# Strassen weight sums on VectorE one at a time, two products accumulated in PSUM, norm weights spread by TensorE: one step of a hybrid encoder on one core

## The chip, the cores and the metric

The kernel runs on one core of a Trainium2 chip. The metric is the device time of one execution in microseconds (us), as a median over runs. A core has engines with instruction queues of their own, which work in order and wait for each other by semaphores: TensorE (PE, matrix products into PSUM), VectorE (DVE), ScalarE (ACT), GpSimd (POOL), and SyncE (SP), which here only issues DMAs from the chip's memory (HBM) to the on-chip memory (SBUF).

## The reference

One inference step of two layers for 512 prompt tokens and 8 x 16 sample tokens, 640 in all, each of 1024 features. Per layer, cut to what matters here:

```python
h = rmsnorm(x) * g_norm[l, 0]
a_x, ..., pu = split(h @ w_in[l])            # four mixers: conv, two attentions, pooling -> o_a .. o_d
for i, o_i in enumerate((o_a, o_b, o_c, o_d)):
    merged += sigmoid(h @ w_gate[l, i] + b_gate[l, i]) * (o_i @ w_branch[l, i])
x = x + rmsnorm(merged @ w_out[l]) * g_norm[l, 1]
gu = (rmsnorm(x) * g_norm[l, 2]) @ w_ffn_in[l]               # 1024 x 5632
x = x + rmsnorm((silu(gu[:, :2816]) * gu[:, 2816:]) @ w_ffn_out[l]) * g_norm[l, 3]
```

All data are fp32.

## The kernel before

**Products in parts.** Every matrix is split in a high and a low part (`split`, `copy` and `sub`), and a product is three matmuls: high x high, high x low, low x high (`dense_k`). A weight chunk arrives by a DMA that SP issues (`w_dma`, two raw tiles of 128x1032 in turn); `w_split` has ScalarE copy the high part (`whi`, L117), and puts the subtraction that gives the low part (`wlo`) in a list, which `flush` gives to VectorE (L274). `whi` and `wlo` have four buffers each, and `w_sub` runs two pieces ahead of the piece that TensorE takes.

**Strassen.** Two stages multiply 2x2 blocks with seven products in place of eight: one of the four gates (`strassen_gates`, four steps n a layer) and the FFN's first matrix (`strassen`, steps j = 3 to 21, 19 a layer; j = 0 to 2 run as plain dense products). A step's blocks are 512 weights x 320 tokens; `product` is 12 matmuls of 320 columns. The weight side needs four sums of blocks for a step: `weight_sums` (L446) forms them on GpSimd, 46 times four in all, one step ahead. The token side needs sums of quadrants, formed once per stage by `token_sums` on VectorE, in ten forms per half; these are put off by `after(delay, ...)` and come out one by one as `tick` counts the matmuls' progress. For the gates they are begun in `prepare_gates` at `f == GATE_F` with the step `GATE_STEP`. The results of a step's products are put together by VectorE's `add`s (L1844 in the FFN, L1538 in the gates), which read one product in PSUM each; ScalarE then applies tanh or Silu.

**Order.** The program's order per engine is the order in which the Python code issues it (`manual_schedule`), so every engine's queue is written out by hand through generators and the hooks named above. Temporary tiles `s` come from 33 slots (`NSLOT`, `alloc`, `free`). PSUM has pools `psD` (two tiles of two banks), `psS` (two), `psT` and `psO` (one each).

**Starts.** `ab_start` begins a dense stage with two chunks whose tokens are not all ready: first the tokens up to `CUT` for both chunks, then those from `CUT`; `hooks` call at a given k of the first halves. It runs four times (input projection and FFN-in of both layers). The very first (`first`) normalises tile by tile of 128 tokens: `norm1` (ScalarE's squares, L344; GpSimd's root, L338; VectorE's scaling by the root and the norm weights g, L353) and `norm2` (TensorE's transposes, L361; ScalarE's high part `Ph`; VectorE's low part `Pl`, L120). The norm weights are brought to all 128 partitions by two DMAs (`load_g`).

Of the kernel before, what the change touches and what calls it, by code (L numbers as in the profile page):

```python
# [25 lines left out]
HT = T // 2  # L26
CUT = 384
NEG = -1e30
BIG = 3.0e38
NSLOT = 33  # L30
ORDER = [0, 1, 2, 3, "v", 4, 5, 6, 7, 12, 13, 9, 10, 14, 11, 15, 8]
# [6 lines left out]
J0 = 3  # L38
GATE_F = 3
GATE_STEP = 0.8  # L40
FO_ORDER = (4, 0, 1, 2, 3, 5, 6, 7, 8, 9, 10)
# [19 lines left out]
def encoder_step(ctx: ExitStack, tc: tile.TileContext, I, O):  # L61
    nc = tc.nc
# [293 lines left out]

    def norm2(xn, hi, lo, t):
        for h in range(2):
            ps = psS()
            for c in range(4):  # L360
                PE.transpose(ps[:, c * 128:(c + 1) * 128], xn[h][:, c * 128:(c + 1) * 128], ident)  # L361
            pv = ps.rearrange("p (c n) -> p c n", c=4)
            split(hi[:, 4 * h:4 * h + 4, t * 128:(t + 1) * 128], lo[:, 4 * h:4 * h + 4, t * 128:(t + 1) * 128], pv)
            free(xn[h])
# [26 lines left out]

    def ab_start(keys, x, hooks, evac_fn):
        w = []
        Ds = [psD(), psD()]
        for i in range(2):
            w.append([w_sub(keys[i], p, 0) for p in range(2)])
            if i == 0:
                w_split(sidx[keys[1], 1])
                flush()
            dense(Ds[i], w[i], x, (0,), hooks[i])  # L400
        for i in range(2):
            dense(Ds[i], w[i], x, (1,))
            evac_fn(i, Ds[i])
            if i == 0:
                w_ahead(keys[1], 1)
                flush()
# [8 lines left out]

    x_first = [load_x(I["x"], t) for t in range(2)]
    g_first = load_g(0, 0)
    ident = const("ident", C_ID, 128)
    mhalf = cpool.tile([128, 8], F32, tag="mhalf", name="mhalf")
    G.memset(mhalf, -0.5)  # L420
# [23 lines left out]
    wsum = {}  # L444

    def weight_sums(key, blocks):  # L446
        a11, a12, a21, a22 = blocks
        s1, s2, s3, s4 = (alloc() for _ in range(4))
        for o, x, y, op in ((s1, a21, a22, ALU.add), (s2, s1[:, :512], a11, ALU.subtract), (s3, a11, a21, ALU.subtract),
                            (s4, a12, s2[:, :512], ALU.subtract)):  # L450
            G.tensor_tensor(out=o[:, :512], in0=x, in1=y, op=op)  # L451
        wsum[key] = (s1, s2, s3, s4)

# [9 lines left out]
    def token_sums(h, dst, at, step=0.6):  # L463
# [12 lines left out]
        def form(n, q):  # L476
            if n == 0:
                t[q] = [alloc() for _ in range(4)]
            i, a, b, op = steps[n]
            o = v2(t[q][i])  # L480
            a = o if a is None else v2(t[q][a]) if isinstance(a, int) else quad(0, *a, q)
            b = v2(t[q][b]) if isinstance(b, int) else quad(*b, q)
            V.tensor_tensor(out=o, in0=a, in1=b, op=op)
            if n == len(steps) - 1:
                t["formed"] = q
# [510 lines left out]
    def layer(l, Htag, Otag, hT, first_units):  # L996
# [471 lines left out]

        def gate_sums(p):
            if p < 4:  # L1470
                weight_sums(("gs", l, p), [t[:, :512] for t in gq["blk", p]])

# [13 lines left out]
        def prepare_gates(f):  # L1486
            if f == 2:
                load_gates(0)
            elif f == GATE_F:
                gq["t2"] = {}  # L1490
# [12 lines left out]
            elif f == 7:  # L1503
                gate_sums(0)
                need(lambda: gq["t"].get("formed") == 1)
# [5 lines left out]
        def strassen_gates(br, branch):  # L1511
# [11 lines left out]

            def product(ps, n, p):
                wh, wl = w_sub(("gs", l, n), p)
# [3 lines left out]
                for k in range(4):  # L1529
                    a, b = wh[:, k * 128:(k + 1) * 128], wl[:, k * 128:(k + 1) * 128]  # L1530
                    for pi, (w, x) in enumerate(((a, xh), (a, xl), (b, xh))):
                        PE.matmul(ps[:, :HT], w, x[k], start=(k == 0 and pi == 0), stop=(k == 3 and pi == 2))  # L1532
                    if k == 1:
                        yield
# [13 lines left out]
            for n in range(4):  # L1548
                f = 2 * n
                ta, tb, X, Y = alloc(), alloc(), alloc(), alloc()  # L1550
                s1, u2, u3, c22 = X[:, :HT], X[:, HT:], Y[:, :HT], Y[:, HT:]
                yield from product(psO(), n, 0)
                copy(s1, out["p"])
# [10 lines left out]
                if pend:  # L1564
                    branch(f - 1, [pend[1]])
                    yield
                yield from product(psT(), n, 3)
                add(c22, out["p"], u3)
                add(u2, out["p"], u2)
                tanh(tb, 1, c22, f + 1)  # L1570
                gate_sums(n + 1)
                yield
                yield from product(psD()[:, 0, :], n, 4)
                add(s1, out["p"], s1)
                tanh(ta, 0, s1, f)
                yield
                yield from product(psD()[:, 0, :], n, 5)
                add(u3, u3, out["p"], ALU.subtract)
                tanh(tb, 0, u3, f + 1)
                yield  # L1580
                yield from product(psS(), n, 6)
                add(u2, out["p"], u2)
                tanh(ta, 1, u2, f)
                post.append(lambda X=X, Y=Y: free(X, Y))
                pend = [ta, tb]
                yield
            for fn in post:
# [197 lines left out]

        def sums(j):
            if j < NJ:
                weight_sums(("fs", l, j), blocks_of(j))

# [18 lines left out]
        for j in range(1, J0):  # L1808
            for g in range(2):
# [4 lines left out]
                if j == J0 - 1 and g == 0:  # L1814
                    sums(J0)
                ev_fi(j, g, Dt)
# [8 lines left out]

        def product(ps, j, p):
            wh, wl = w_sub(("fs", l, j), p)
            xh, xl = moving[p]
            for k in range(4):
                a, b = wh[:, k * 128:(k + 1) * 128], wl[:, k * 128:(k + 1) * 128]  # L1830
                for pi, (w, x) in enumerate(((a, xh), (a, xl), (b, xh))):
                    PE.matmul(ps[:, :HT], w, x[k], start=(k == 0 and pi == 0), stop=(k == 3 and pi == 2))  # L1832
                if k == 1:
# [4 lines left out]
        def strassen(j):  # L1838
# [6 lines left out]

            p1 = product(psO(), j, 0)
            for fn in tail[:1]:
# [8 lines left out]
            add(u3, p7, u2)  # L1856
            sums(j + 1)
            p5 = product(psT(), j, 3)
            add(c22, p5, u3)
            add(u2, p5, u2)  # L1860
            p2 = product(psD()[:, 0, :], j, 4)
            add(s1, p2, s1)
            A.activation(out=act[:, :HT], in_=s1, func=AF.Silu)  # L1863
            p4 = product(psD()[:, 0, :], j, 5)
# [3 lines left out]
            add(act[:, :HT], act[:, :HT], s1, ALU.mult)  # L1868
            p3 = product(psS(), j, 6)
            add(u2, p3, u2)  # L1870
# [59 lines left out]
    with tc.manual_schedule():  # L1930
        h0 = (big("Ph"), big("Pl"))

        def first(evac_fn):
            xn = {}
            turned = lambda t: norm2(xn.pop(t), h0[0], h0[1], t)
            def normed(t):
                xn[t] = norm1(x_first[t], g_first)
                free(*x_first[t])

            normed(0)  # L1940
            normed(1)
            turned(0)
            normed(2)
            turned(1)
            w_split(1)
            flush(G)
            turned(2)
            normed(3)

            def mid():  # L1950
                normed(4)
                turned(3)

            ab_start([("in", 0, c) for c in ORDER[:2]], h0, ({4: mid}, {6: lambda: turned(4)}), evac_fn)
            free(*g_first)
# [154 lines left out]
```

## Time and profile before

| | |
|---|---|
| median of 3 runs | 2091.82 us (2089.9 to 2094.06) |
| the profiled execution's own time | 2095.22 us |
| its span, first to last instruction | 2093.4 us |
| mean granted TensorE clock | 0.993 of full |
| TensorE busy | 2038.4 us (97%) |
| VectorE busy | 1491.2 us (71%) |
| ScalarE busy | 981.7 us (47%) |
| GpSimd busy | 429.6 us (21%) |
| HBM traffic | 101 GB/s over the span |

The busy shares say how much of the span an engine worked; a view of waits says for which instruction of which engine it stood idle. In a row, `wlo<-raw,whi` reads: tile `wlo` is written from `raw` and `whi`; buffer numbers are left out. The gates' Strassen stages lie near 476 to 560 us (layer 0) and 1511 to 1590 (layer 1), the FFN's of layer 1 from 1694 to 1934.

### The profile page before, as it was taken

What the parts mean: (1) busy time and instruction counts of PE and PEld (TensorE: products, weight loads), DVE (VectorE), ACT (ScalarE), POOL (GpSimd) and SP (SyncE); (2) the same over time, 40 slices, a digit from 0 to 9 for tenths busy, and PEclk for the clock granted to TensorE, in tenths of its full rate; (3) what the DMA queues carried; (4) which work ended last, traced back from release to release, by engine and by line L of the source; (5) the groups of instructions that cost most, each with busy time, mean ns of one, the idle gap of its engine ahead of it and who ended that gap; (6) DMA issues with size and microseconds to landing.
All of it is one profiled execution on the core that took longest, in us unless ns stands there. A gap on an engine that the chain in (4) does not pass through costs nothing. (4 is left out here: it accounts for less than half of the span.)

```text
span 2093.4 us, 34625 instructions
## 1 busy us (share of the span) xinstructions
PE 2038.4 (97%) x13050; PEld 1928.6 (92%) x13050; DVE 1491.2 (71%) x2914; ACT 981.7 (47%) x2100; POOL 429.6 (21%) x450
## 2 busy tenths in 40 slices
PE   7999999998999999999999999999999999999998
PEld 7999999998989999988889999999988899999887
DVE  5687478698769889853375774876986698888432
ACT  5656355554444344343256553555544443444431
POOL 3211000113013444400040100001130234443000
PEclk9999999999999999999999999999999999999999
DMA  4312244342341222222523122444313422221223
GB/s 148 109 62 79 81 146 140 119 134 73 102 168 62 91 88 84 81 81 71 171 82 110 68 77 82 151 151 141 111 46 130 153 71 90 88 82 61 101 91 121
DMA packets 100743, 214.35 MB, mean 102 GB/s; under 512 B 10896, under 2 KB 35056, under 8 KB 100576
## 3 DMA queue, kind: packets, MB, share of 16 engines
q1 hardware_dynamic: 99552, 209.16, 29.9%
q0 software_dynamic: 1024, 2.98, 0.4%
q8 instruction: 102, 1.67, 0.3%
q14 instruction: 65, 0.53, 0.1%
HBM read 196.02 MB, written 16.08 MB: 101 GB/s over the span
## 5 line engine op out<-in xcount | busy, mean ns | idle before, releaser
L274 DVE TENSOR_TENSOR wlo<-raw,whi 128x512 fp32r<-128x512 f32 (+2 forms) x388 | 267.5, 694 | 160.0 <-ACT whi L117 155.5
L117 ACT ACTIVATE whi<-raw 128x512 fp32r<-128x512 f32 (+2 forms) x390 | 230.5, 606 | 168.6 <-issue 70.6
L274 DVE TENSOR_TENSOR wlo<-s,whi 128x512 fp32r<-128x512 f32 x196 | 205.3, 1048 | 17.5 <-ACT whi L117 16.1
L117 ACT ACTIVATE s<-s 128x512 fp32r<-128x512 f32 (+7 forms) x294 | 175.0, 619 | 77.6 <-DVE s L1420 45.6
L376 PE MATMUL D<-Ph,whi 128*128 128x320 f32 (+2 forms) x736 | 176.9, 315 | 0.9 <-DVE s L1412 0.9
L376 PE MATMUL D<-Qh,whi 128*128 128x320 f32 (+2 forms) x736 | 176.0, 313 | 0.9 <-DVE s L1412 0.9
L376 PE MATMUL D<-Pl,whi 128*128 128x320 f32 (+2 forms) x736 | 173.6, 310 | 0.0
L376 PE MATMUL D<-Ph,wlo 128*128 128x320 f32 (+2 forms) x736 | 173.6, 310 | 0.0
L376 PE MATMUL D<-Qh,wlo 128*128 128x320 f32 (+2 forms) x736 | 172.8, 309 | 0.0
L376 PE MATMUL D<-Ql,whi 128*128 128x320 f32 (+2 forms) x736 | 172.8, 309 | 0.0
L117 ACT ACTIVATE whi<-s 128x512 fp32r<-128x512 f32 x196 | 117.2, 621 | 42.2 <-PE S L1832 18.9
L338 POOL TENSOR_TENSOR r<-ms,mhalf 128x1 f32<-128x1 f32 x40 | 22.0, 551 | 542.1 <-DVE ms L1672 470.4
L376 PEld LDWEIGHTS D<-Ph,whi 128*128 128x128 f32 x736 | 123.0, 189 | 3.6 <-DVE s L1412 1.4
L376 PEld LDWEIGHTS D<-Pl,whi 128*128 128x128 f32 x736 | 125.2, 189 | 0.6 <-DVE Pl L120 0.4
L376 PEld LDWEIGHTS D<-Qh,whi 128*128 128x128 f32 x736 | 122.5, 188 | 3.4 <-DVE s L1412 1.5
L376 PEld LDWEIGHTS D<-Ql,whi 128*128 128x128 f32 x736 | 124.7, 188 | 0.2
L376 PEld LDWEIGHTS D<-Ph,wlo 128*128 128x128 f32 x736 | 124.8, 189 | 0.0
L376 PEld LDWEIGHTS D<-Qh,wlo 128*128 128x128 f32 x736 | 124.3, 188 | 0.0
L744 POOL CAST s<-s 128x16 fp32r<-128x16 f32 x128 | 30.8, 264 | 407.5 <-DVE s L1420 98.2
L451 POOL TENSOR_TENSOR s<-V,V 128x512 f32<-128x512 f32 x48 | 76.1, 1584 | 172.5 <-DMA V<-in_w_fi 85.3
L117 ACT ACTIVATE s<-T 128x320 fp32r<-128x320 f32 (+6 forms) x132 | 50.9, 386 | 106.5 <-PE T L515 62.5
L1863 ACT ACTIVATE s<-s 128x320 f32<-128x320 f32 x38 | 17.9, 472 | 148.4 <-DVE s L1844 148.4
(480 smaller groups left out, 5890.5 us busy)
## 6 DMA issues: line engine op xcount, KB each, us to landing
raw<-in_w_gate SPq DMA_DIRECT2D x48, 512.0 KB, 3.6
raw<-in_w_fi SPq DMA_DIRECT2D x48, 512.0 KB, 3.5
raw<-in_w_fo SPq DMA_DIRECT2D x44, 512.0 KB, 3.5
V<-in_w_fi SPq DMA_DIRECT2D x80, 256.0 KB, 3.0
raw<-in_w_in SPq DMA_DIRECT2D x32, 512.0 KB, 3.3
s<-in_ck_d SPq DMA_DIRECT2D x32, 256.0 KB, 4.1
s<-in_cv_d SPq DMA_DIRECT2D x32, 256.0 KB, 4.1
s<-in_ck_f SPq DMA_DIRECT2D x32, 256.0 KB, 4.1
```

The source lines that it names most:

```text
L117: A.activation(out=out, in_=in_, func=AF.Copy, scale=scale)
L274: E.tensor_tensor(out=lo, in0=raw, in1=hi, op=ALU.subtract)
L338: G.tensor_tensor(out=out, in0=ssum, in1=mhalf[:, :n], op=ALU.pow)
L376: PE.matmul(Dt[:, h, :c1 - c0], a, b[:, k, c0:c1], start=(start and pi == 0), stop=(stop and pi == 2))
L451: G.tensor_tensor(out=o[:, :512], in0=x, in1=y, op=op)
L744: G.tensor_copy(out=dst[:, 512:KEYS], in_=f32(src[:, 16 * b:16 * b + 16]))
L1863: A.activation(out=act[:, :HT], in_=s1, func=AF.Silu)
```

## The change

1. `weight_sums` becomes `weight_sum(key, blocks, i)`: one sum at a time, on VectorE. In the FFN they are issued behind the adds of products p7 and p5, behind the product p2 and the adds of p4; those of the first step j = 3 are put off by `after(1.0 + i)` within the last dense chunk before. In the gates they come behind products 3 to 6, and the first step's four at `f == 7`.
2. Product 4 is accumulated onto product 0 in the `psO` tile, and product 6 onto product 3 in the `psT` tile. In each step two adds go, and ScalarE reads PSUM for one half.
3. In `first` the norm weights of layer 0 come as two rows of 2 KB, issued by ScalarE's queue; a memset of `ones` and two matmuls spread them into a `psD` tile `gp`. Tiles 0 and 1 are scaled from `gp`; ScalarE copies it to SBUF for the rest. The order of tiles, transposes and weight splits changes.
4. `CUT` 384 to 256, for all four `ab_start`s.
5. `GATE_F` 3 to 2, `GATE_STEP` 0.8 to 1.0. Slots of the token sums are taken one by one; `NSLOT` 33 to 36; the software DMA's scratch is set to 8192.

```diff
-CUT = 384
+CUT = 256
-NSLOT = 33
+NSLOT = 36
-GATE_F = 3
-GATE_STEP = 0.8
+GATE_F = 2
+GATE_STEP = 1.0
...
-    x_first = [load_x(I["x"], t) for t in range(2)]
-    g_first = load_g(0, 0)
+    g_first = [alloc(), alloc()]
+    for h in range(2):
+        A.dma_start(out=g_first[h][:1, :512], in_=gbc[0, 0:1, h * 512:(h + 1) * 512])
+    ones = cpool.tile([1, 128], F32, tag="ones", name="ones")
+    G.memset(ones, 1.0)
+    x_first = [load_x(I["x"], 0)]
     ident = const("ident", C_ID, 128)
+    x_first.append(load_x(I["x"], 1))
+    gp = psD()
+    for h in range(2):
+        PE.matmul(gp[:, h, :], ones, g_first[h][:1, :512], start=True, stop=True)
...
+    def weight_sum(key, blocks, i):
+        a11, a12, a21, a22 = blocks
+        s = wsum.setdefault(key, {})
+        s[i] = alloc()
+        x, y, op = ((a21, a22, ALU.add), (s[0][:, :512], a11, ALU.subtract), (a11, a21, ALU.subtract),
+                    (a12, s[min(i, 1)][:, :512], ALU.subtract))[i]
+        V.tensor_tensor(out=s[i][:, :512], in0=x, in1=y, op=op)
+
     def weight_sums(key, blocks):
-        a11, a12, a21, a22 = blocks
-        s1, s2, s3, s4 = (alloc() for _ in range(4))
-        for o, x, y, op in ((s1, a21, a22, ALU.add), (s2, s1[:, :512], a11, ALU.subtract), (s3, a11, a21, ALU.subtract),
-                            (s4, a12, s2[:, :512], ALU.subtract)):
-            G.tensor_tensor(out=o[:, :512], in0=x, in1=y, op=op)
-        wsum[key] = (s1, s2, s3, s4)
+        for i in range(4):
+            weight_sum(key, blocks, i)
...
-                        PE.matmul(ps[:, :HT], w, x[k], start=(k == 0 and pi == 0), stop=(k == 3 and pi == 2))
+                        PE.matmul(ps[:, :HT], w, x[k], start=(not more and k == 0 and pi == 0), stop=(k == 3 and pi == 2), skip_group_check=more)
...
-                if j == J0 - 1 and g == 0:
-                    sums(J0)
+                    for i in range(4):
+                        after(1.0 + i, lambda i=i: sums(J0, i))
...
-            p1 = product(psO(), j, 0)
+            pa, pb = psO(), psT()
+            p1 = product(pa, j, 0)
...
             add(u3, p7, u2)
-            sums(j + 1)
-            p5 = product(psT(), j, 3)
+            sums(j + 1, 0)
+            p5 = product(pb, j, 3)
             add(c22, p5, u3)
-            add(u2, p5, u2)
-            p2 = product(psD()[:, 0, :], j, 4)
-            add(s1, p2, s1)
-            A.activation(out=act[:, :HT], in_=s1, func=AF.Silu)
+            sums(j + 1, 1)
+            p2 = product(pa, j, 4, True)
+            A.activation(out=act[:, :HT], in_=p2, func=AF.Silu)
+            sums(j + 1, 2)
             p4 = product(psD()[:, 0, :], j, 5)
...
             add(act[:, :HT], act[:, :HT], s1, ALU.mult)
-            p3 = product(psS(), j, 6)
+            sums(j + 1, 3)
+            p3 = product(pb, j, 6, True)
             add(u2, p3, u2)
...
+            for h in range(2):
+                copy(g_first[h][:, :512], gp[:, h, :])
             turned(0)
+            w_split(0)
+            flush()
+            turned(1, (psT, psO))
             normed(2)
-            turned(1)
-            w_split(1)
-            flush(G)
-            turned(2)
             normed(3)
...
-            ab_start([("in", 0, c) for c in ORDER[:2]], h0, ({4: mid}, {6: lambda: turned(4)}), evac_fn)
+            ab_start([("in", 0, c) for c in ORDER[:2]], h0, ({3: lambda: turned(2)}, {4: mid}), evac_fn, lambda: turned(4))
```

The line numbers of the changed kernel are higher than those of the kernel before: L462 is the sum in `weight_sum`, L1426 was L1412, L1434 was L1420, L497 was L483, L1553 was L1538, L1787 was L1770, L1862 was L1844.

VectorE's queue where the first gate's Strassen step begins in layer 0, before (a `wlo` of a product whose weights are a sum reads `s`; `V` are raw weight blocks):

```order
L1412 SCALAR_TENSOR_TENSOR s_6137<-s_6137,D_6195 128x640
L1420 TENSOR_TENSOR s_4713<-s_4713,s_6137 128x640
L120 TENSOR_TENSOR s_6159<-s_5948,s_6158 128x640
L274 TENSOR_TENSOR wlo_6226<-s_6178,whi_6225 128x512
L274 TENSOR_TENSOR wlo_6248<-s_6176,whi_6247 128x512
L1538 TENSOR_TENSOR s_6222<-S_6246,s_6222 128x320
L120 TENSOR_TENSOR Ql_141<-s_6269,Qh_140 128x2x128
L274 TENSOR_TENSOR wlo_6282<-V_5431,whi_6281 128x512
```

and in the changed kernel, from the last product of a branch to the same place:

```order
L1426 SCALAR_TENSOR_TENSOR s_6022<-s_6022,D_6153 128x640
L1434 TENSOR_TENSOR s_4380<-s_4380,s_6022 128x640
L462 TENSOR_TENSOR s_6183<-V_5439,V_5440 128x512
L462 TENSOR_TENSOR s_6185<-s_6183,V_5437 128x512
L462 TENSOR_TENSOR s_6187<-V_5437,V_5439 128x512
L462 TENSOR_TENSOR s_6189<-V_5438,s_6185 128x512
L120 TENSOR_TENSOR Pl_140<-s_5604,Ph_139 128x320 x2
L120 TENSOR_TENSOR Pl_140<-s_5992,Ph_139 128x320 x2
L274 TENSOR_TENSOR wlo_6200<-s_6185,whi_6199 128x512
L1426 SCALAR_TENSOR_TENSOR s_6144<-s_6144,D_6202 128x640
L120 TENSOR_TENSOR s_6148<-s_6058,s_6147 128x640
L274 TENSOR_TENSOR wlo_6233<-s_6187,whi_6232 128x512
```

The four sums stand behind L1426, which reads a branch product in `D`, and in front of the four `Pl` pieces (x2 and x2) and the first `wlo` that reads a sum.

VectorE's queue where the FFN's Strassen steps begin in layer 0 (j = 3), before:

```order
L274 TENSOR_TENSOR wlo_7936<-V_7542,whi_7935 128x512
L120 TENSOR_TENSOR Pl_7541<-s_7829,Ph_7540 128x640
L120 TENSOR_TENSOR Pl_7541<-s_7830,Ph_7540 128x640
L274 TENSOR_TENSOR wlo_7967<-s_7923,whi_7966 128x512
L1770 TENSOR_TENSOR s_7930<-D_7934,s_7930 128x640
L274 TENSOR_TENSOR wlo_8000<-s_7924,whi_7999 128x512
L274 TENSOR_TENSOR wlo_8018<-s_7922,whi_8017 128x512
L1844 TENSOR_TENSOR s_7996<-S_8016,s_7996 128x320
L274 TENSOR_TENSOR wlo_8036<-V_7543,whi_8035 128x512
L1844 TENSOR_TENSOR s_7997<-S_8034,s_7996 128x320
L274 TENSOR_TENSOR wlo_8062<-V_7545,whi_8061 128x512
L1844 TENSOR_TENSOR s_7997<-T_8060,s_7997 128x320
```

and in the changed kernel:

```order
L274 TENSOR_TENSOR wlo_7919<-V_7533,whi_7918 128x512
L120 TENSOR_TENSOR Pl_7532<-s_7876,Ph_7531 128x640
L462 TENSOR_TENSOR s_7930<-V_7535,V_7536 128x512
L120 TENSOR_TENSOR Pl_7532<-s_7861,Ph_7531 128x640
L462 TENSOR_TENSOR s_7945<-s_7930,V_7533 128x512
L274 TENSOR_TENSOR wlo_7954<-s_7945,whi_7953 128x512
L462 TENSOR_TENSOR s_7963<-V_7533,V_7535 128x512
L462 TENSOR_TENSOR s_7977<-V_7534,s_7945 128x512
L1787 TENSOR_TENSOR s_7913<-D_7917,s_7913 128x640
L274 TENSOR_TENSOR wlo_7992<-s_7963,whi_7991 128x512
L274 TENSOR_TENSOR wlo_8010<-s_7930,whi_8009 128x512
L1862 TENSOR_TENSOR s_7987<-S_8008,s_7987 128x320
```

The four sums of j = 3, which stood in GpSimd's queue, lie among the last `Pl` of the token sums and the `wlo` of the first three products.

ScalarE's queue at the start of the program, from the squares of tile 0, before:

```order
L344 ACTIVATE s_150,st_149<-s_88 128x512 [waits DMAHW0_49]
L344 ACTIVATE s_150,st_149<-s_90 128x512 [waits DMAHW1_49,Activation_49]
L344 ACTIVATE s_162,st_161<-s_92 128x512 [waits DMAHW2_49]
L344 ACTIVATE s_162,st_161<-s_94 128x512 [waits DMAHW3_49,Activation_49]
L117 ACTIVATE Ph_134<-S_173 128x4x128 [waits PE_49]
L117 ACTIVATE Ph_134<-S_180 128x4x128 [waits PE_49]
L344 ACTIVATE s_188,st_187<-s_106 128x512 [waits DMAHW7_49]
L344 ACTIVATE s_188,st_187<-s_108 128x512 [waits DMAHW0_49,Activation_49]
L117 ACTIVATE Ph_134<-S_199 128x4x128 [waits PE_49]
```

and in the changed kernel:

```order
L344 ACTIVATE s_155,st_154<-s_94 128x512 [waits DMAHW1_49]
L344 ACTIVATE s_155,st_154<-s_96 128x512 [waits DMAHW3_49,Activation_49]
L344 ACTIVATE s_167,st_166<-s_100 128x512 [waits DMAHW5_49]
L344 ACTIVATE s_167,st_166<-s_102 128x512 [waits DMAHW6_49,Activation_49]
L117 ACTIVATE s_88<-D_104 128x512 [waits DMAHW0_49,DVE_49,PE_49]
L117 ACTIVATE s_89<-D_104 128x512 [waits DMAHW2_49,PE_49]
L117 ACTIVATE Ph_139<-S_180 128x4x128 [waits PE_49]
L117 ACTIVATE Ph_139<-S_187 128x4x128 [waits PE_49]
L117 ACTIVATE whi_194<-raw_115 128x512 [waits DMAHW1_49]
```

Two copies out of the tile `D` that holds the spread norm weights now stand ahead of the first `Ph`, and the first of them waits for VectorE.

## Rows read from the trace of the kernel before

**Rows 1.** The page, part 1: busy time, share and instructions of each engine.

```profile
PE 2038.4 (97%) x13050; PEld 1928.6 (92%) x13050; DVE 1491.2 (71%) x2914; ACT 981.7 (47%) x2100; POOL 429.6 (21%) x450
```

**Rows 2.** Waits of TensorE: us in total, times, longest us.

```profile
PE S L1532 <- DVE wlo L274: 6.3, 3, 3.5
PE S L1832 <- DVE wlo L274: 4.7, 11, 0.5
...
PE O L803 <- DVE s L788: 4.2, 2, 2.1
...
PE T L1532 <- DVE wlo L274: 2.6, 4, 0.7
...
PE D L1532 <- DVE wlo L274: 0.8, 2, 0.4
```

**Rows 3.** Timeline, TensorE, gates: start us, us, engine, line, operation.

```profile
481.20 0.31 PE L1532 MATMUL O<-Pl,whi 128*128 128x320 f32 x1
...
481.93 0.31 PE L1532 MATMUL S<-Qh,whi 128*128 128x320 f32 x1
```

**Rows 4.** Timeline, GpSimd, VectorE, TensorE at the first gate; idle before in brackets.

```profile
483.38 6.58 POOL L451 TENSOR_TENSOR s<-s,s 128x512 f32<-128x512 f32 x4 [8.60 <-DMA s<-in_w_gate]
...
487.07 3.43 DVE L274 TENSOR_TENSOR wlo<-s,whi 128x512 fp32r<-128x512 f32 x2
...
488.88 0.63 PE L1532 MATMUL S<-s,wlo 128*128 128x320 f32 x1 [3.51 <-DVE wlo L274]
489.31 0.73 PE L1532 MATMUL S<-s,whi 128*128 128x320 f32 x2
...
490.11 0.74 PE L1532 MATMUL S<-s,whi 128*128 128x320 f32 x2
```

**Rows 5.** Windows: us, busy of PE, PEld, DVE, ACT, POOL, clock, DMA, GB/s.

```profile
488.20:494.90 6.70, 6.02 (x22) 6.02 (x23) 4.73 (x7) 0.66 (x2) 1.76 (x2) 0.50 0.26 91
...
sum 16.70, PE 15.07 PEld 15.07 DVE 13.04 ACT 5.92 POOL 3.79; mean PE 5.02 PEld 5.02 DVE 4.35 ACT 1.97 POOL 1.26
...
1660.00:1694.00 34.00, 34.00 (x243) 33.93 (x242) 29.57 (x42) 15.09 (x25) 5.31 (x5) 1.00 0.18 63
1694.00:1934.00 240.00, 237.13 (x1599) 234.03 (x1598) 209.68 (x304) 97.58 (x189) 114.98 (x72) 1.00 0.24 80
```

**Rows 6.** Groups by line and form, VectorE: busy us, mean ns, idle before.

```profile
L274 DVE TENSOR_TENSOR wlo<-raw,whi 128x512 fp32r<-128x512 f32 x340 | 238.8, 707 | 157.1 <-ACT whi L117 152.9 <-PE D L376 3.8
```

**Rows 7.** Timeline, VectorE: a form beside GpSimd's sums, then undisturbed instructions.

```profile
473.58 1.89 DVE L483 TENSOR_TENSOR s<-s,Pl 128x640 f32<-128x640 f32 x1
...
1684.78 0.69 DVE L274 TENSOR_TENSOR wlo<-raw,whi 128x512 fp32r<-128x512 f32 x1
1685.38 0.82 DVE L483 TENSOR_TENSOR s<-s,Pl 128x640 f32<-128x640 f32 x1
```

**Rows 8.** Timeline, VectorE and TensorE, the last tile at layer 1's FFN start.

```profile
1655.84 1.42 DVE L353 SCALAR_TENSOR_TENSOR s<-s,r,s 128x512 f32<-128x512 f32 x2 [0.73 <-POOL r L338]
...
1658.61 1.03 PE L361 MATMUL S<-ident,s 128*128 128x128 f32 x8
```

**Rows 9.** Timeline, start of the program: ScalarE, VectorE, TensorE, TensorE.

```profile
7.89 0.63 ACT L344 ACTIVATE s<-s 128x512 f32<-128x512 f32 x1 [1.66 <-DMA s<-in_x]
...
9.73 1.42 DVE L353 SCALAR_TENSOR_TENSOR s<-s,r,s 128x512 f32<-128x512 f32 x2 [4.43 <-DMA s<-in_g_norm]
...
19.32 0.69 PE L376 MATMUL D<-Ph,whi 128*128 128x384 f32 x1
...
37.69 0.45 PE L376 MATMUL D<-Ph,whi 128*128 128x320 f32 x2
```

**Rows 10.** Waits of VectorE, one row; timeline, GpSimd and VectorE, an even FFN step.

```profile
DVE V L1646 <- ACT s L1647: 3.3, 4, 0.8
...
1795.12 1.57 POOL L451 TENSOR_TENSOR s<-raw 128x512 f32<-128x512 f32 x1 [7.62 <-DMA raw<-in_w_fi]
...
1802.07 0.48 DVE L1844 TENSOR_TENSOR s<-S,s 128x320 f32<-128x320 f32 x1
```

## What the change was predicted to do

> **What bounds the kernel now.** The page's first part comes first: TensorE is busy 97% of the span, VectorE 71%, GpSimd 21% [rows 1]. So only the 55 us in which TensorE is idle, and what a lower clock costs, can be won; an instruction less on another engine counts only where TensorE waits for that engine. The second view is TensorE's waits [rows 2]. Those that the diff can reach end on VectorE: for the low halves `wlo` of split weights in the gates' Strassen products (L1532: 6.3 + 2.6 + 0.8 us), for a low half of the attention units just ahead of them (L803: 4.2 us), and in the FFN's products (L1832). The third view is the order in time. A product is 12 matmuls of 320 columns, one each 0.146 us (five from 481.20 to 481.93) [rows 3], so 1.76 us. At the first gate GpSimd runs four weight sums in a row, 6.58 us; in that time VectorE's two `wlo` take 3.43 us and TensorE waits 3.51 us [rows 4]. Afterwards matmuls start 0.267 us apart (three from 489.31 to 490.11) instead of 0.146, in a stretch whose granted clock is 0.50, the lower of the two levels (1.2 of 2.4 GHz) [rows 4, 5]. There are three such stretches in the gates, 15.07 us of TensorE's time together [rows 5]; at the full rate that is 15.07 x 0.146/0.267 = 8.2, so 6.9 us are lost to the clock.
>
> **The sums' own price.** `weight_sums` leaves GpSimd (184 instructions, 46 groups of four) and comes to VectorE. VectorE shows no 128x512 sum of two SBUF fp32 tiles into a third; the nearest row is `wlo<-raw`, same size and two SBUF inputs: 707 ns on average [rows 6], at a pitch of 0.60 where nothing disturbs it (from 1684.78 to the next start at 1685.38) [rows 7]. The other end is GpSimd's 1.64 us for the same sum [rows 4]. I take 0.60, the nearer in engine and shape. The average of 707 and the 1.89 us of a 128x640 sum at 473.58 (0.82 at 1685.38) [rows 7] come from times when GpSimd sums too; with GpSimd's sums gone I expect these stretchings gone.
>
> **FFN-in.** One Strassen step j is seven products, 12.3 us. From 1694 to 1934 the profile shows TensorE with 1599 matmuls [rows 5], the 19 x 84 = 1596 of this stage and three more. At 0.146 to 0.147 each the stage needs 233.0 to 234.6 of its 240.0 us; I take 233.7, so 6.3 us are lost a layer, 12.6 in two. (The waits listed for L1832 are less, since a matmul's modelled end covers the first part of each wait.) VectorE's work per j before: seven `wlo` at 0.60 and nine adds at 0.40 (a row of 0.48 [rows 10], next start 0.40 later) = 7.8 us, and by its busy time 209.68/240 it takes 87% [rows 5], 10.7 of 12.3, so some 3 us a j are stretching. After: the two accumulated products take out 2 adds (76 here, 16 in the gates), four sums come in: 4.2 + 2.8 + 2.4 = 9.4 us of 12.3. Each `wlo` is two products ahead of its use, and TensorE's queue has room. I let 11.6 of the 12.6 go. New is the start of the stage: from 1660 to 1694 VectorE is at 29.57 of 34 us [rows 5], and four sums (2.4 us) for j=3 come to stand there, which GpSimd formed beside it. By the order they stand in between the `wlo` of the first three products, so that the third's is late by about 0.8, the second's by 0.4: 1.2 a layer, 2.4 in two. Bounds: nothing, and 2 x 2.4 + 2 x 2.0 if the clock falls too. Together -11.6 + 2.4 = -9.2.
>
> The sums now stand in an in-order queue behind which `wlo` is queued, so a late weight would stop both. For the even steps the weights came at 1795.12, when GpSimd's sum was released by the DMA; VectorE comes to the place of that sum just behind p7's add at 1802.07 [rows 10], 7 us later. This cover is why I cost that wait at nothing.
>
> **Gates.** Waits that go: L803 4.2 us, because the token sums start one f earlier and the 1.9 us forms ahead of L788 shrink to 0.8 (the last of them at 473.58) [rows 2, 7]; S L1532 6.3, T 2.6, D 0.8 [rows 2]: 13.9. I leave 2.6 of it standing (TensorE's T products follow small transposes and copies that stay) and take all 6.9 of clock, since no wait over 1 us is left to bring the clock down. New: in the first gate the four sums stand behind an instruction that waits for a branch product (L1426 in the order), to about 473.8, then 2.4 us of sums and 1.6 of `Pl`, so the second product's `wlo` comes at about 480.0 where TensorE wants it at 479.8; up to 0.8 a layer, 1.6. Later gates: VectorE has about 14.8 us of work for nine product-long units (15.8 us), 94%; the smallest margin that I find walking through the order is 0.5 us. Term: -13.9 + 2.6 - 6.9 + 1.6 = -16.6. Bounds: -20.8 (everything goes) and -8 (half).
>
> **CUT 384 to 256.** The first halves of the two first chunks get shorter by 128 columns, 0.058 us a matmul (0.146 x 128/320); 24 + 18 matmuls stand before the last tile's transposes, so these are reached 2.4 us earlier. In the FFN-in of layer 1 they ran at 1658.61 [rows 8] and would be due at 1656.2, but their input is normalised from 1655.84 to 1657.26: about 0.7 us of new wait, in three of the four places, +2.1. Bounds: 0 and 3 x 1.4.
>
> **The start.** VectorE's first scaling waits until 9.73 us for the norm weights' spreading DMAs [rows 9]. Two rows of 2 KB by ScalarE's queue and two matmuls replace them. VectorE had by then stood idle for 4.43 us, so tile 0's scaling may start up to 4.4 us earlier; tile 1's second half lands only for 7.89 [rows 9], its scaling ends near 10. The order then has a new chain: ScalarE's two copies of `gp` to SBUF come before its first `Ph`, and they wait for VectorE's sixth instruction, the last reader of that PSUM tile. They run from about 10.6 to 11.9, `Ph` ends at 13, and the first dense matmul comes near 13.5 instead of 19.32 [rows 9]. But it comes with tiles 2 to 4 unready: waits of about 1.5 (tile 2's scaling), 0.5 (`wlo`) and 0.8 (`then=turned(4)` has no matmul left to cover it), and matmuls at the lower clock in between. By this the second halves end between 36.5 and 38.4, before 37.69 [rows 9]: I take 0, bounds -4 and +3.
>
> That engines take turns at a PSUM tile is seen in this trace: VectorE's L1646 waits for ScalarE's L1647 on the same tile, four times, 3.3 us [rows 10]. The Trainium skill, page "PSUM — Partial Sum Buffer", section "PSUM bank collisions raise a hardware error", states that two engines must not touch one bank in the same partitions at one time, two readers included, and that the program has to keep them apart. By that rule the copies can't move beside VectorE's scaling, and the start's term is my 0; without it they would be done by 7 and the term would be the bound of -4.
>
> **No cost:** GpSimd's few software DMAs with a smaller scratch, three slots more, the ident load moved one place up in SP's queue (its landing is covered by tile 0's statistics).
>
> **Sum.** -9.2 - 16.6 + 2.1 + 0 = -23.7 us on the profiled execution's 2095.2: 2071.5. That execution lies 3.4 us above the median of 2091.8, so the median becomes about 2068.
>
> **Rivals.**
> A. VectorE becomes the bound in the gates. For: 94% by my count, an in-order queue that waits for branch products. Against: the stretched instructions are a third shorter without GpSimd's sums. Half of both gains is then left: -8.3 - 4.6 + 2.1 = -10.8, a median of 2081.
> B. All the waits go and the start gains too: -20.8 - 12.6 - 4 + 0 = -37.4, 2054. For: every large wait has the same cause. Against: the new places at the stage starts.
> C. Slower: a sum on VectorE costs what it costs on GpSimd. From 0.60 + 2.9/4 = 1.33 us a sum (2.9 us of VectorE's time are free per j) VectorE sets the pace. At 1.64 a j takes 9.4 - 2.4 + 6.6 = 13.6 instead of 240/19 = 12.6: 38 x 1.0 = +38; in the gates 14.8 + 4.2 = 19 against 15.8 and eight times: +26. Some 2155. For: such sums did take 1.9 us beside GpSimd [rows 7]. Against: this company ends.
> D. The change doesn't do what it says for the time: the waits for `wlo` were ScalarE's `whi` or DMAs, and only their name changes: 2095 + 2 = a median of 2094. Against: 3.43 us for two `wlo` in [rows 4].
>
> **Chances.** Forecast 0.55 (2058 to 2077), A 0.2, B 0.13, C 0.05, D 0.07. No change means within 0.2%, 4.2 us, about what a measurement of this kernel can tell. Faster: forecast, A and B, 0.88; the same: most of D, 0.06; slower: C and the rest of D, 0.06. The range for 8 in 10 leaves out the far half of B and C and D: 2055 to 2086.
>
> **What would show it.** Right: no GpSimd sum, S L1532 waits under 1 us each, granted clock 1.00 all through the gates, L803 without a wait, sums on VectorE near 0.68 us, one j at 12.3 to 12.4 us. Wrong: sums over 1 us; VectorE waiting for a DMA at a sum; stretches at 0.50 in the gates; the second halves of the start ending after 40 us, which would eat the gates' gain; T4 waits of over 1.5 us at the three later starts.

## The result, and the profile after

| | before | after |
|---|---|---|
| median | 2092.07 us (4 runs) | 2066.34 us (2065.11 to 2068.54, 4 runs) |
| ratio, 95% interval | | 0.9878 [0.9861, 0.9896] |
| span of the profiled execution | 2093.4 us | 2066.8 us |

Predicted were 2068 us, 2055 to 2086. The page of the changed kernel, part 1, has GpSimd at a third of [rows 1]:

```profile
PE 2031.8 (98%) x13054; PEld 1923.9 (93%) x13054; DVE 1438.4 (70%) x3008; ACT 990.1 (48%) x2102; POOL 139.6 (7%) x265
```

VectorE is busy 53 us less, though it has 92 instructions more by the program (184 sums more, 92 adds fewer). The groups by line say why; first the one row of before that [rows 6] did not hold, then the changed kernel's (busy us, mean ns):

```profile
L274 DVE TENSOR_TENSOR wlo<-s,whi 128x512 fp32r<-128x512 f32 x196 | 205.3, 1048 | 17.5 <-ACT whi L117 16.1
```
```profile
L274 DVE TENSOR_TENSOR wlo<-raw,whi 128x512 fp32r<-128x512 f32 x342 | 237.1, 698 | 152.5 <-ACT whi L117 152.0
L274 DVE TENSOR_TENSOR wlo<-s,whi 128x512 fp32r<-128x512 f32 x196 | 134.2, 686 | 48.0 <-ACT whi L117 48.0
...
L462 DVE TENSOR_TENSOR s<-V,V 128x512 f32<-128x512 f32 x48 | 32.8, 684 | 0.0
```

The `wlo` of summed weights fell from 1048 to 686 ns, and a sum costs 684 ns on VectorE, where "near 0.68" was forecast; the next start comes 0.60 later (478.85, then 479.45 below), the value that the sum was worked out with. TensorE's waits after, to be held against [rows 2]:

```profile
PE S L361 <- DVE s L353: 6.0, 6, 2.3
PE O L1283 <- DVE wlo L274: 4.2, 2, 2.1
PE D L376 <- DVE s L1426: 3.5, 4, 1.9
PE S L1547 <- DVE wlo L274: 2.4, 2, 1.2
...
PE S L1850 <- DVE wlo L274: 1.4, 4, 0.5
```

Of the gates' 13.9 us one wait of 1.2 a layer is left. The first gate in layer 0 after (VectorE's sums, then TensorE's wait behind them), against [rows 4]:

```profile
476.92 0.69 DVE L462 TENSOR_TENSOR s<-V,V 128x512 f32<-128x512 f32 x1
...
478.85 0.69 DVE L462 TENSOR_TENSOR s<-V,s 128x512 f32<-128x512 f32 x1
479.45 1.69 DVE L120 TENSOR_TENSOR Pl<-s,Ph 128x320 fp32r<-128x320 f32 x4
...
481.80 0.42 PE L1547 MATMUL S<-Qh,wlo 128*128 128x320 f32 x1 [1.20 <-DVE wlo L274]
```

Windows after: layer 0's gates, layer 1's FFN steps (against [rows 5]), and a stretch near the start:

```profile
475.00:545.00 70.00, 68.80 (x460) 66.88 (x460) 59.60 (x104) 37.43 (x81) 0.00 (x0) 1.00 0.21 70
...
1671.00:1911.00 240.00, 239.00 (x1618) 237.26 (x1617) 193.30 (x348) 104.63 (x197) 0.00 (x0) 1.00 0.24 83
57.00:63.00 6.00, 5.64 (x34) 5.65 (x35) 5.78 (x11) 2.60 (x5) 2.29 (x2) 0.72 0.27 88
```

VectorE works 193 us of 240 where it worked 210, with the sums. The half clock is gone from the gates (granted clock 1.00 here, and in layer 1 from 1500 to 1570), but the last window has a new one: 0.72 on average, 0.50 from 58.5 to 61.5, the lower of the two levels. It stands behind a wait of 2.1 us (L1283).

Where the time went is read by finding the same matmul in both traces. Each row is the stretch up to the matmul of that time in the trace of before, and how much more (+) or less (-) the changed kernel needed for it. Each kernel has one trace, and the same matmuls can shift by 1 to 2 us from one kernel's trace to the next where no edit reaches them, so small rows are read with the runs below:

| stretch, up to (before / after) | us | predicted |
|---|---|---|
| start, 70.91 / 70.67 | -0.2 | 0 |
| units ahead of the gates, layer 0, 472.79 / 473.36 | +0.8 | 0 |
| gates, layer 0, 554.83 / 544.64 | -10.8 | -8.3 |
| start of the FFN, tokens, 637.21 / 627.79 | +0.8 | +0.7 |
| dense part and first FFN step, 677.27 / 669.16 | +1.3 | +1.2 |
| FFN steps, layer 0, 921.55 / 906.76 | -6.7 | -5.8 |
| start of layer 1, 1082.33 / 1068.36 | +0.8 | +0.7 |
| units ahead of the gates, layer 1, 1483.93 / 1471.07 | +1.1 | 0 |
| gates, layer 1, 1604.93 / 1581.55 | -10.5 | -8.3 |
| start of the FFN, 1666.28 / 1643.51 | +0.6 | +0.7 |
| dense part and first FFN step, 1706.72 / 1685.47 | +1.5 | +1.2 |
| FFN steps, layer 1, 1936.32 / 1909.60 | -5.5 | -5.8 |
| sum | -26.7 | -23.7 |

### The profile page after: what moved, and what is told of

Same layout as the page of the kernel before. It is cut to its first block, busy times and chain, and to the rows that moved or that the text cites. A ratio compares the mean times of both kernels' runs of the same rounds, so it can differ in the third digit from the quotient of the medians.

```text
span 2066.8 us, 34314 instructions
## 1 busy us (share of the span) xinstructions
PE 2031.8 (98%) x13054; PEld 1923.9 (93%) x13054; DVE 1438.4 (70%) x3008; ACT 990.1 (48%) x2102; POOL 139.6 (7%) x265
## 4 chain that ended last, share of the span: by engine, by line
PE 84%; DVE 8%; ACT 2%; issue 2%; POOL 2%; DMA 1%; SPq 0%; DVEq 0%; POOLq 0%; ACTq 0%
PE D L376 25%; PE D L1644 11%; PE T L1850 6%; PE O L1850 6%; PE S L1850 6%; PE D L1422 4%; PE T L1644 3%; PE O L1644 3%; PE D L1850 3%; PE D L1283 2%; PE O L817 1%; PE T L1547 1%; PE S L1547 1%; PE O L1547 1%; DVE wlo L274 1%
## 5 line engine op out<-in xcount | busy, mean ns | idle before, releaser
L274 DVE TENSOR_TENSOR wlo<-raw,whi 128x512 fp32r<-128x512 f32 (+2 forms) x390 | 261.4, 675 | 155.0 <-ACT whi L117 154.2
L274 DVE TENSOR_TENSOR wlo<-s,whi 128x512 fp32r<-128x512 f32 x196 | 134.2, 686 | 48.0 <-ACT whi L117 48.0
L117 ACT ACTIVATE whi<-s 128x512 fp32r<-128x512 f32 x196 | 121.9, 626 | 56.7 <-PE S L1850 40.7
L117 ACT ACTIVATE s<-O 32x64 f32<-32x64 f32 (+1 forms) x174 | 47.7, 274 | 84.5 <-PE O L817 67.2
L1644 PE MATMUL D<-whi,s 128*128 128x512 f32 x240 | 81.5, 394 | 0.0
L1426 DVE SCALAR_TENSOR_TENSOR s<-s,D 128x640 f32<-128x640 f32 x64 | 52.3, 817 | 38.4 <-PE D L1422 38.4
```

The source lines that it names most:

```text
L117: A.activation(out=out, in_=in_, func=AF.Copy, scale=scale)
L274: E.tensor_tensor(out=lo, in0=raw, in1=hi, op=ALU.subtract)
L1426: V.scalar_tensor_tensor(out=v2(tg[b]), in0=v2(tg[b]), scalar=1.0, in1=Dt[:, :, :HT], op0=ALU.add, op1=ALU.mult)
L1644: PE.matmul(ps, a, b, start=(first and pi == 0), stop=(last and pi == 2))
```

## The experiments

All are edits of the changed kernel unless said otherwise. Their ratios stand to runs of before on the same chip. The first four undo or alter one part each.

**Sums on GpSimd.**

```diff
-        V.tensor_tensor(out=s[i][:, :512], in0=x, in1=y, op=op)
+        G.tensor_tensor(out=s[i][:, :512], in0=x, in1=y, op=op)
```

> The changed kernel with one edit: its weight sums are issued to GpSimd again, at the places where the changed kernel has them. Theory (GpSimd's sums stretch VectorE's instructions with two SBUF inputs, and that made the waits): wlo<-s is back at about 1.0 us on average (0.69 in the changed kernel), L1547 and L1850 wait again for wlo, the clock falls in the gates again; 2080 to 2092 us. Rival (the two adds less a step and the finer order made the gain): wlo's duration does not matter, 2066 to 2070 us.

Measured: 2067.42 us, 0.9882 [0.9865, 0.9899], the rival's number, and yet the stretching is back, as the groups of this kernel show:

```profile
L274 DVE TENSOR_TENSOR wlo<-s,whi 128x512 fp32r<-128x512 f32 x196 | 193.3, 986 | 32.5 <-ACT whi L117 31.7
```

So the stretching alone does not make the waits. The theory in its simple form fell.

**The two adds back.**

```diff
-            p2 = product(pa, j, 4, True)
-            A.activation(out=act[:, :HT], in_=p2, func=AF.Silu)
+            p2 = product(psD()[:, 0, :], j, 4)
+            add(s1, p2, s1)
+            A.activation(out=act[:, :HT], in_=s1, func=AF.Silu)
```

(with `add(u2, p5, u2)` and product 6 in `psS`, and the same in the gates)

> The changed kernel without the accumulation in PSUM: products 4 and 6 have tiles of their own again and the two adds a step are back (92 in all), the sums stay on VectorE. Theory: VectorE has room for them in the FFN (10.2 of 12.3 us a step), little in the gates (about 15.6 of 15.8): 2066 to 2071 us. Rival (the accumulation made the gain): 2080 us or more.

Measured: 2066.51 us, 0.9873 [0.9858, 0.9887]. With the sums on VectorE the accumulation is worth nothing.

**Gates' token sums late.**

```diff
-GATE_F = 2
-GATE_STEP = 1.0
+GATE_F = 3
+GATE_STEP = 0.8
```

> The changed kernel with GATE_F and GATE_STEP of before (3 and 0.8): the gates' token sums start one f later. Theory: the new waits for L1426 ahead of the gates (2.2 us in both layers) go, L817 waits for a low half by at most 1 us a layer since the forms are no longer stretched; 2064 to 2068 us. Rival (the earlier start is what removed the wait of L803 before): waits of about 2 us a layer at L817, with the clock falling behind them, 2070 to 2076 us.

Measured: 2066.01 us, 0.9873 [0.9857, 0.9889], within the theory's bounds, but not by its reason: the waits on L1426 stay at 3.0 us in four (3.5 in the changed kernel), so the earlier token sums did not cause them. The run with the old start, below, bears on what did.

**CUT.** The three later starts at 384 again (`CUT` becomes a value that the program sets to 384 behind the first start).

```diff
             ab_start([("in", 0, c) for c in ORDER[:2]], h0, ({3: lambda: turned(2)}, {4: mid}), evac_fn, lambda: turned(4))
+            CUTS[0] = 384
```

> The changed kernel with CUT 256 for the very first start alone and 384 for the three later starts. Theory: these three starts lost 0.85 to 0.96 us each by the shorter first halves, so 2.6 us come back: 2063.7 us. Rival (the loss there comes from something else, such as the sums of the first step): within 1 us of 2066.3.

Measured: 2063.44 us, 0.9859 [0.9844, 0.9874]: CUT costs what the trace says. Within each of the three starts the same matmuls fall back by 0.8 to 1.0 us against the kernel before in all ten kernels here that have 256 there, and by 0.0 in the three that have 384.

Three of these edits (the sums', the adds', the token sums') each cost under 1.2 us when undone. The next four runs undo them in pairs, and all three, with the diffs above.

**Sums on GpSimd and the two adds back.**

> The changed kernel with the sums on GpSimd again and the two adds a step back; the gates' token sums still start early (GATE_F 2). Each of these edits alone cost under 1.2 us. Theory (a wait needs both the stretched instructions and the fuller queue; either edit alone takes the wait away): the FFN loses about 6 us a layer again, the gates 2 to 4 in all; 2078 to 2084 us. Rival (the parts add up, and the gain lies elsewhere): 2067 to 2069 us.

Measured: 2076.86 us, 0.9932 [0.9921, 0.9944], 1.1 us under the expected range. The FFN loses again, L1852 (L1850 of the changed kernel) waits for `wlo` 13 times, 6.5 us. The FFN of layer 0, first with GpSimd's sums (this kernel), then with VectorE's (the kernel with the two adds back):

```profile
650.00:890.00 240.00, 236.82 (x1594) 233.65 (x1593) 208.25 (x304) 97.80 (x189) 113.06 (x72) 1.00 0.24 79
```
```profile
650.00:890.00 240.00, 239.26 (x1618) 237.46 (x1618) 206.47 (x386) 101.84 (x197) 0.00 (x0) 1.00 0.26 83
```

VectorE is busy longer without the sums, in 304 instructions, than with them, in 386.

**Sums on GpSimd and the token sums late.**

> The changed kernel with the sums on GpSimd again and GATE_F, GATE_STEP of before; the accumulation in PSUM stays. Theory: the FFN keeps its gain (a loss of about 1 us a layer as with the sums on GpSimd alone), and at the first gate the waits of 2 to 4 us and the half clock behind them return in both layers; 2078 to 2086 us. Rival (the parts add up): 2066 to 2069 us.

Measured: 2075.22 us, 0.9923 [0.9911, 0.9935], under the theory's range and far over the rival's. The FFN has no wait, the first gate has its old one (against [rows 4]):

```profile
487.27 0.41 PE L1547 MATMUL S<-s,wlo 128*128 128x320 f32 x1 [3.33 <-DVE wlo L274]
```

**The two adds back and the token sums late**, so that of the three the sums' move alone is left.

> The changed kernel with the two adds a step back and GATE_F 3, GATE_STEP 0.8; the sums stay on VectorE. Theory: without GpSimd's sums nothing is stretched, so the sums' move alone carries the gain: 2065 to 2069 us, low-half waits under 1.5 us each. Rival (at least two of the three edits are needed): over 2075 us.

Measured: 2066.59 us, 0.9882 [0.9869, 0.9895]. Of the three edits the sums' move alone carries the whole gain.

**All three back.**

> The changed kernel with all three back: sums on GpSimd, two more adds a step, GATE_F 3 and GATE_STEP 0.8. What is left of the change is the start, CUT 256 and three slots more. Theory: the time of before and the 2.6 us that CUT costs, 2092 to 2096 us. Rival (the slots or the order of single sums make part of the gain): under 2088 us.

Measured: 2087.0 us, 0.9981 [0.9972, 0.999]: a gain of 4 us is left where a loss of 2.6 was expected. By the traces it lies in the gates (4.2 and 4.4 us a layer), with none of the three edits. Against this run the matched matmuls also say what each edit does by itself, in two layers together: the accumulation takes 11.5 us off the FFN's steps and 0.5 off the gates; the earlier token sums 1.7 and 9.2; the sums' move 14.4 and 10.5. So with GpSimd's sums left in place one of the two lesser edits frees the FFN and the other the gates, and the two together come to the same 2067 us as the sums' move alone. GpSimd's sums for layer 0's first gate, before and in this kernel:

```profile
469.62 1.41 POOL L451 TENSOR_TENSOR s<-V,V 128x512 f32<-128x512 f32 x1 [2.96 <-DVE s L1420]
473.18 1.59 POOL L451 TENSOR_TENSOR s<-V,s 128x512 f32<-128x512 f32 x1 [2.15 <-DVE s L753]
```
```profile
467.17 1.85 POOL L462 TENSOR_TENSOR s<-V,V 128x512 f32<-128x512 f32 x1
468.98 1.73 POOL L462 TENSOR_TENSOR s<-V,s 128x512 f32<-128x512 f32 x1
```

Before, two sums waited for VectorE to be done with a slot, and so fell among the forms just ahead of L803. That was tried alone, on the kernel before:

```diff
-NSLOT = 33
+NSLOT = 36
...
-            if n == 0:
-                t[q] = [alloc() for _ in range(4)]
             i, a, b, op = steps[n]
+            if a is not None:
+                t.setdefault(q, {})[i] = alloc()
```

(and the DMA scratch of 8192)

> The kernel before with the change's slots alone: 36 in place of 33, those of the token sums taken one by one, and the smaller DMA scratch. Theory (what is left of the gain without the three main edits, 2087.0 against 2091.4 us and 2.6 us for CUT, comes from slots: GpSimd's sums for the first gate waited for them at 469.62 and 473.18 us and fell on the forms that TensorE waited for): these two waits of GpSimd go, 2084 to 2089 us. Rival (it comes from the sums being issued one by one): 2091 to 2093 us.

Measured: 2087.02 us, 0.9981 [0.9972, 0.999]. Both waits of GpSimd are gone, and L803 waits 2.1 us in two where it waited 4.2. So the slots, which the prediction put at no cost, are worth 3.7 us to the kernel before (2090.7 to 2087.02), the three more and the taking one by one together. What they are worth with the sums on VectorE no run shows. The run with all three edits undone gains 4.4 us (2091.39 to 2087.0) and has paid CUT's 2.5 out of that, so some 3 us of its gain stay unexplained; each of the two ratios is known to about 1.9 us.

**The start of before** (CUT 384 there, 256 later).

```diff
-            for h in range(2):
-                copy(g_first[h][:, :512], gp[:, h, :])
             turned(0)
-            w_split(0)
-            flush()
-            turned(1, (psT, psO))
             normed(2)
+            turned(1)
+            w_split(1)
+            flush(G)
+            turned(2)
             normed(3)
```

(with `load_g` and the hooks of before)

> The changed kernel with the start of the kernel before (the norm weights spread by two DMAs, the old order of tiles, CUT 384 there) and CUT 256 for the three later starts. Theory (the new start gains 1.8 us to 51 us and pays 1.6 of it for a stretch at half the clock from 58 us on): matmuls near 51 us come 1.8 us later than in the changed kernel, no half clock near 58 us, 2066 to 2068 us. Rival (the new start gains its 1.8 us for good, the half clock has nothing to do with it): 2068 to 2070 us with the half clock there too.

Measured: 2065.93 us, 0.9884 [0.987, 0.9897]: no difference. By the traces matmuls at 57 us come 0.8 us later than in the changed kernel, and the half clock near 60 us is there too:

```profile
58.00:64.00 6.00, 5.82 (x36) 5.82 (x37) 5.76 (x11) 2.78 (x5) 2.11 (x2) 0.72 0.26 88
```

So the new start is not its cause, and the expected 1.8 us were 0.8. In the kernel before, the wait of 2.1 us at L1269 (L1283 after), which stands ahead of it, has no half clock behind it (1.00 from 58.5 to 64.5). What decides that is open.

TensorE's wait for the branch products (L1412 before, L1426 after) is short again here. The rows of the kernel before, of this kernel (L1419), and of the kernel with all three edits undone, which keeps the new start:

```profile
PE D L376 <- DVE s L1412: 1.9, 4, 0.7
```
```profile
PE D L376 <- DVE s L1419: 2.0, 4, 0.8
```
```profile
PE D L376 <- DVE s L1426: 2.9, 4, 1.8
```

The longest wait is 0.6 to 0.8 us in the three kernels with the old start, and 1.7 to 2.0 in ten of the eleven with the new one (1.0 in the other, sums on GpSimd and the two adds back). So the longer wait goes with the new start and not with the three edits; by what path is open.

**Does GpSimd's reading do it, or its lateness?** The kernel with the two adds back, and sums that deliver nothing:

```diff
+            if j + 1 < NJ:
+                bl, dd = blocks_of(j + 1), alloc()
+                for q in range(4):
+                    G.tensor_tensor(out=dd[:, :512], in0=bl[q], in1=bl[(q + 1) % 4], op=ALU.add)
+                free(dd)
             sums(j + 1, 0)
```

> The kernel of e2 (sums on VectorE, the two adds a step back, 2066.5 us) with four extra sums a step on GpSimd in the FFN, of the same weight blocks, written to a slot that nobody reads: work that delivers nothing. Theory (GpSimd's reading of SBUF stretches VectorE's instructions with two SBUF inputs): in the FFN wlo<-s is near 1.0 us instead of 0.69, a step needs more of VectorE than the 12.3 us it has (10.2 and some 3 of stretching), so TensorE waits in nearly every step; 2080 to 2105 us. Rival (in the kernels with GpSimd's sums, TensorE waited because these sums came late): wlo as in e2, 2066 to 2069 us.

Measured: 2180.73 us, 1.0427 [1.0404, 1.0449]. The groups of 700 to 880 us:

```profile
L274 DVE TENSOR_TENSOR wlo<-s,whi 128x512 fp32r<-128x512 f32 x47 | 44.0, 935 | 9.4 <-ACT whi L117 9.4
L1864 DVE TENSOR_TENSOR s<-S,s 128x320 f32<-128x320 f32 x36 | 17.4, 484 | 7.4 <-PE S L1852 7.4
...
L462 DVE TENSOR_TENSOR s<-V,s 128x512 f32<-128x512 f32 x6 | 10.6, 1768 | 0.0
```

Nobody reads these sums, and from 650 to 890, in layer 0's FFN, VectorE waits for no DMA and for nothing of GpSimd's:

```profile
DVE wlo L274 <- ACT whi L117: 13.4, 18, 0.8
DVE s L1864 <- PE S L1852: 8.9, 8, 1.3
```

Still a VectorE instruction with two SBUF inputs takes up to 1.77 us, while one that reads PSUM and SBUF stays at 484 ns. The same `wlo` is slow beside a GpSimd sum and quick behind it (VectorE's rows, then GpSimd's, which is idle from 744.84 to 752.09):

```profile
743.64 1.74 DVE L274 TENSOR_TENSOR wlo<-s,whi 128x512 fp32r<-128x512 f32 x1
...
747.17 0.69 DVE L274 TENSOR_TENSOR wlo<-s,whi 128x512 fp32r<-128x512 f32 x1 [0.78 <-ACT whi L117]
```
```profile
743.25 1.59 POOL L1881 TENSOR_TENSOR s<-raw,raw 128x512 f32<-128x512 f32 x1
752.09 4.70 POOL L1881 TENSOR_TENSOR s<-V,V 128x512 f32<-128x512 f32 x3 [7.26 <-DMA V<-in_w_fi]
```

The trace of the kernel before says the same of its own sums: of the 196 `wlo<-s`, the 111 that had a GpSimd sum beside them for at least half of their time took 1329 ns on average and the 80 that had none 681; adds that read `S` in PSUM took 480 and 481. The mechanism is shown; its price (114 us, where 38 was the upper end expected) is three times what I had allowed. The Trainium skill, page "SBUF — State Buffer", section "Who interferes with whom", states that a VectorE instruction with two SBUF inputs contends with a GpSimd instruction that reads SBUF, and that one with at most one SBUF input, outside the 2-port perf modes, does not: the two rows, 1768 and 484 ns, agree. A step takes 15.4 us (layer 0's 19 steps take 291.8 us, 235.3 in the kernel with the two adds back), and VectorE is busy 90% of the time from 700 to 800. Behind TensorE's waits the half clock comes too, in eight stretches of layer 0's 19 steps (mean granted clock 0.95 from 650 to 890).

**A better version.** CUT as in the fourth run, and the first step's four sums of each stage on GpSimd:

```diff
-                weight_sum(("fs", l, j), blocks_of(j), i)
+                weight_sum(("fs", l, j), blocks_of(j), i, G if j == J0 else V)
...
-                        after(1.0 + i, lambda i=i: sums(J0, i))
+                        sums(J0, i)
```

(and `G if p == 0 else V` for the gates; the last argument is the engine)

> A version from the runs so far: CUT 256 in the first start alone, and the four weight sums of the first Strassen step of each stage on GpSimd, where VectorE is full, the others on VectorE. Theory: the FFN starts lose 1.3 to 1.5 us less a layer, the waits of 1.2 us at the second gate product go, on top of 2063.4 us: 2057 to 2060 us. Rival (GpSimd's sums stretch the forms beside them by as much as they take off): 2062 to 2065 us.

Measured: 2056.88 us, 0.9839 [0.9825, 0.9852], just under the expected range and the fastest of all: 9.5 us under the changed kernel by the medians, 8 by the ratios. By the matched matmuls, against the changed kernel, the first FFN step gives back 1.5 us a layer and the gates 1.4 to 1.5; the rest is mostly CUT. GpSimd forms the FFN's four sums as soon as the blocks have landed, 30 us before they are wanted:

```profile
612.70 1.29 POOL L463 TENSOR_TENSOR s<-V,V 128x512 f32<-128x512 f32 x1 [5.06 <-DMA V<-in_w_fi]
614.07 1.29 POOL L463 TENSOR_TENSOR s<-s,V 128x512 f32<-128x512 f32 x1
615.31 1.30 POOL L463 TENSOR_TENSOR s<-V,V 128x512 f32<-128x512 f32 x1
616.56 1.30 POOL L463 TENSOR_TENSOR s<-V,s 128x512 f32<-128x512 f32 x1
```

## Why the prediction was right

**The sums' price.** Right: 684 ns, 0.60 from start to start, and the stretching went with GpSimd's sums. The run with sums that deliver nothing shows the cause apart from their lateness.

**FFN.** Right in size: -12.15 + 2.83 = -9.3 against -11.6 + 2.4 = -9.2. The working gave two reasons side by side, the stretching and the two adds; the runs show that either one is enough (with the sums alone back on GpSimd 1.1 and 0.5 us are lost in the steps, with the adds alone back nothing) and that only both undone bring the waits back. The cost at the stage's start is that of the first step's four sums: it is gone where GpSimd forms them.

**Gates.** The mechanism was right, the size short: -21.3 against -16.6, just beyond the bound of -20.8. The 2.6 us for T products that I left standing went too. What made those waits is not shown: they are also gone in the kernel before with the change's slots alone, where GpSimd still forms the sums and the waits at `S` grow from 6.3 to 7.5 us. The new wait behind the sums is 1.2 us a layer by the list of waits, 1.4 with the part that the matmul's end covers, where 0.8 was the most that I allowed; the granted clock stays at 1.00 behind it. VectorE is busy 85% of the gates (59.60 of 70 us from 475 to 545), where the count by hand said 94%. The credit to the earlier token sums for L803's wait was wrong in the changed kernel: with `GATE_F` of before the time is the same and no wait for L802 (L788 before) is listed. Only beside GpSimd's sums do the earlier token sums take it away (2.0 to 2.1 us without them, none with).

**Ahead of the gates.** Missed in layer 1: +1.1, one wait of 1.9 us for L1426 where 0.7 stood before; it goes with the new start, as the rows of the run with the old one show. Layer 0's +0.8 is scatter: the other kernels that change the same things have -0.3 to +0.3 there.

**CUT.** Right: 0.8 us in each of three starts of the changed kernel, and 2.9 us less in all with it undone (2063.44 against 2066.34). The working is less exact than its result: 2.4 us earlier against the 1.35 of room from 1657.26 to 1658.61 makes 1.05, not the 0.7 taken.

**The start.** Right at 0 (-0.2 at 71 us), but in part by luck. The path is nearly as worked out; the rows after, VectorE's scalings, ScalarE's copies, TensorE's first dense matmul and the end of the second halves (35.89), are to be held against [rows 9]:

```profile
6.05 1.41 DVE L353 SCALAR_TENSOR_TENSOR s<-s,r,D 128x512 f32<-128x512 f32 x2 [0.80 <-POOL r L338]
...
8.77 1.41 DVE L353 SCALAR_TENSOR_TENSOR s<-s,r,D 128x512 f32<-128x512 f32 x2 [0.66 <-POOL r L338]
...
10.26 1.08 ACT L117 ACTIVATE s<-D 128x512 f32<-128x512 f32 x2 [2.40 <-issue]
...
13.38 0.58 PE L376 MATMUL D<-Ph,whi 128*128 128x256 f32 x1 [1.83 <-ACT Ph L117]
...
35.89 0.46 PE L376 MATMUL D<-Ph,whi 128*128 128x320 f32 x2
```

The first dense matmul comes 5.9 us earlier and the second halves end 1.8 us earlier, at 35.89, outside the 36.5 to 38.4 that was worked out; the half clock at 58 us, which the prediction did not have, took 1.6 of that. Part of the 1.8 is scatter: the eleven kernels with the new start reach this matmul between 35.8 and 37.0, the three with the old between 36.7 and 37.7. The copies wait until VectorE's scalings from `gp` are done (8.77 + 1.41 = 10.18). The Trainium skill, page "PSUM — Partial Sum Buffer", section "PSUM bank collisions raise a hardware error", states that the program has to keep two readers of a bank apart; the order here, 10.26 behind 10.18, agrees, and no run shows what a breach would do.

**No cost: slots.** Wrong for the kernel before (3.7 us). In the sum it is likely without weight, since the sums that waited for slots left GpSimd; no run tries the changed kernel with 33.

**Rivals.** A and C did not come: the gates' low halves come in time but for the one wait of 1.2 us a layer, and a sum takes 684 ns, not 1.64 us. D fell, as the waits for `wlo` went and the time with them. B came true for the gates alone.

That the time came out is no proof of the sums' move by itself: with the sums back on GpSimd the other two edits still bring 2067.42 us. What proves it is the run with the sums' move alone (2066.59) and the one with sums that deliver nothing.

## What to carry to other kernels

An engine with a low busy share can still be what is too slow: read whether the same instruction takes longer in some stretches than in others, and which engine works beside it then. When several edits of one change each cost nothing if undone, undo them in pairs before calling any of them idle: here one alone (the sums' move) gives the whole gain, and the two others together give it too, but add nothing to it. Work that is moved to a full engine for this reason can stay where it was in the stretches where the other engine is far ahead.

## What was not expected of the hardware

Four sums a step on GpSimd whose result nobody reads cost 114 us (2066.5 to 2180.7), when VectorE had 10.6 of 12.3 us of work of its own (206.47 us busy in 240). A wait of about 2 us on TensorE was followed by a stretch at half the clock (1.2 of 2.4 GHz) in some kernels and not in others at the same place, so 1.6 us come and go with edits elsewhere.
